# Use lags of blocks that go through DRAM, and the order of token-major products, in a two-layer hybrid trunk

## The chip, the core and the metric

The kernel runs on one core of one Trainium2 chip, in one launch. The metric is the device time in microseconds (us) from the start to the end of the program. TensorE (PE in the profile; its weight loads are PEld) multiplies, VectorE (DVE), ScalarE (ACT) and GpSimd (POOL) do the elementwise work, SyncE (SP) issues most DMAs. Each engine works through its own queue in order.

## What is computed

A trunk of two layers on 256 tokens of width 2048, in fp32. Cut to what matters:

```
h = x
for i in range(2):
    hn = rmsnorm(h, norm[i])
    if i == 0:                       # even layer
        u = hn @ e_w_in              # 2048 x 6144
        ya = head_rmsnorm(hgrn2(q, f, v), a_norm) * silu(za)   # gated linear recurrence, 8 heads
        yb = rg_lru(causal_conv(xb)) * silu(zb)                # 1024 channels
        mix = concat(ya, yb) @ e_w_out                         # 2048 x 2048
    else:                            # odd layer
        u = hn @ o_w_in              # 2048 x 8208
        yc = head_rmsnorm(mlstm(silu(conv(q, k)), v, gates), c_norm)
        mix = (yc * sigmoid(og) * silu(z)) @ o_w_out           # 2048 x 2048
    h = h + mix
    pl = rmsnorm(p[i] @ ple_w[i], ple_norm[i])
    h = h + sigmoid(h @ ple_gate_w[i]) * pl                    # 2048 x 2048
return rmsnorm(h, final_norm)
```

Nearly all the arithmetic is in the products with large weight matrices.

## The kernel before

**Products.** Each fp32 operand is split into two parts of a shorter format (fp32r): `hi` is a cast and `lo` the rest. A product takes three matmuls: hi x hi, hi x lo, lo x hi. The weights are split on the fly. `load_weights` (L119) takes a tile of 128 x 2048, in two halves of 1024 columns: SP loads `raw` (5 buffers), ACT casts it to `whi` (L131), DVE subtracts to get `wlo` (L132). `whi` and `wlo` have 4 buffers each, so two tiles of weights are ready or in work at a time. The split instructions have a raised priority.

There are two layouts. `block` (L154) makes a feature-major result of 128 features x 256 tokens: 32 products per block, one bank of PSUM, the weights stationary. `quarter_tok` (L214) is a quarter of a token-major chunk of 512 features x 256 tokens: the activations are stationary (128 x 128), the weights stream by (512 columns), and there are two accumulators, one for each half of the tokens (`hf`). A quarter `kq` covers four blocks of the contraction (`kk`, 128 rows each), and kk 0, 1 lie in the first half of the weight tile, kk 2, 3 in the second. With 2 token halves, 4 blocks and 3 matmuls that is 24 matmuls of 512 columns per quarter, 96 per chunk. Before the change both halves of a quarter run one after the other: all of hf 0, then all of hf 1. The result of block k and of its activations sits in `act[k // 2]`, an entry for two blocks of the contraction; such entries come from a pool `ap` with 12 buffers, tag `ahl`.

`project_tok` (L190) runs a chunk's four quarters in order. `project_two` (L199) runs the first two chunks of a stage together, in the order (0,0), (0,1), (0,2), (1,0), (1,1), (1,2), (0,3), (1,3) of (chunk, quarter), so that the last quarter of the contraction is needed late. The accumulators of `project_tok` and of the first chunk of `project_two` come from the PSUM pool `pm` (3 banks, tag `mm`); those of the second chunk come from `px` (3 banks, tag `mx`), which small products share. A chunk takes two banks. The token-major stages, in order, with their chunks: ei 2, ez 2 and eo 4 (even layer), g0 4 (its embedding gate), ov 4, oog 4, oz 4, oo 4 (odd layer), g1 3 (its embedding gate, whose last chunk is made otherwise, L1167). That is 31 chunks. g0, ov and g1 begin with `project_two`.

**What reads the accumulators.** ei: ACT L772. ez and oz: ACT L556, then DVE L557. eo and oo: DVE L420. g0: ACT L432. ov: ACT L976. oog: ACT L1096. g1: ACT L1146. The projected embeddings ahead of ei and of oo (`embed`, L317) are evicted by L347 and L349.

**Turning blocks from token-major to feature-major.** A result that becomes the next stage's input must be transposed. `to_features` (L377) and `feature_major` (L515) do this for a chunk of 512 features: DVE transposes 32 x 32 squares (L382, L520), then `across` (L504) writes the tile to DRAM on POOL's queue (L507) and reads it back in four pieces that put the squares in place (L510); after that ACT and DVE scale and split it (L390, L398, L400, L527, L145, L146). `to_features` serves the residual stream: names dfe (after eo, read by g0), dfg (after g0, read by ov and the stages behind it) and dfo (after oo, read by g1). `feature_major` serves the mixer's output: duan (two chunks of the even layer, read by eo) and ducn (three of the odd layer, read by oo; the fourth is transposed by PE).

**The order of work.** Side work is written as generators in named lanes. `pump` (L74) moves each lane one step on, and puts what the step issues behind the latest matmul, cast, subtraction and hop on the queue of each engine (`issue_after`). `quarter_tok` pumps once, in its middle, after 12 matmuls; `block` once, between L161 and L167. `across` ends with `lag` empty steps, so the use of a block stands that many pumps behind its departure. Where a stage must have an entry, `ready` (L406) steps the lane until it is there, and `drain` (L81) runs a lane to its end. Within these bounds a scheduler lays out each queue at build time, by priority and by when it takes operands to be ready.

In the even layer the second `feature_major` (lane fm1) starts ahead of the second gate block pair (`gate_mul`, L849, which evicts through L299 to L305); eo's second quarter reads its entries y[2] and y[3]. In `out_proj` (L413) and `ple_gate` (L425) the last block's entries are read by the quarters (0,3) and (1,3) of the next stage's `project_two`. `ple_gain` (L371, POOL's L374) runs in a lane during eo.

Of the kernel before, what the change touches and what calls it, by code (L numbers as in the profile page):

```python
# [22 lines left out]
KT = D // P  # L23
# [20 lines left out]
def trunk(ctx: ExitStack, tc: tile.TileContext, a, out):  # L44
    nc = tc.nc
    v, s, gp, te, sy = nc.vector, nc.scalar, nc.gpsimd, nc.tensor, nc.sync
# [14 lines left out]
    last = {}  # L61
# [12 lines left out]
    def pump():  # L74
        with ExitStack() as behind:
            for ins in last.values():
                behind.enter_context(tc.issue_after(ins))
            for lane in list(lanes):
                step(lane)
# [31 lines left out]
    def pc(name, i=0, n=None):  # L111
        o, w = PRM[name]
        return prm[:, o + i:o + i + (n or 1)]
# [5 lines left out]
    def load_weights(src, pieces=(1, 1), queues=(sy,)):  # L119
        parts = []  # L120
        for hf in range(2):
            raw = wp.tile([P, 1024], F32, name="raw", tag="raw", bufs=5)
            hi = wp.tile([P, 1024], F32R, name="whi", tag="whi")
            lo = wp.tile([P, 1024], F32R, name="wlo", tag="wlo")
            n = 1024 // pieces[hf]
            for c in range(0, 1024, n):
                r, h, l = (x[:, c:c + n] for x in (raw, hi, lo))
                queues[c // n % len(queues)].dma_start(out=r, in_=src[:, hf * 1024 + c:hf * 1024 + c + n])
                with ExitStack() as order:
                    order.enter_context(tc.high_priority(offset=400))  # L130
                    last["act"] = s.copy(h, r).ins  # L131
                    last["dve"] = v.tensor_tensor(out=l, in0=r, in1=h.bitcast(F32), op=ALU.subtract).ins  # L132
            parts.append((hi, lo))
        return parts

    def act_pair():

        x = ap.tile([P, 1024], F32R, name="ahl", tag="ahl")
        x4 = x.rearrange("p (k i t) -> p k i t", i=2, k=2)
        return x4[:, :, 0], x4[:, :, 1], x  # L140

    def split_act(src, name):
        hi, lo, both = act_pair()
        src = src.rearrange("p (k t) -> p k t", k=2)
        (v.tensor_copy if name == "p0" else s.copy)(hi, src)  # L145
        v.tensor_tensor(out=lo, in0=src, in1=hi.bitcast(F32), op=ALU.subtract)  # L146
        return hi, lo, both
# [39 lines left out]
    def tokens(x, k, hf):  # L187
        return x[:, k, hf * P:(hf + 1) * P]

    def project_tok(w, j, act, before=None):  # L190

        ps = [pm.tile([P, 512], F32, name="mm", tag="mm") for _ in range(2)]
        for kq in range(4):
            if before is not None:
                before(kq)
            quarter_tok(w, j, kq, act, ps)
        return ps
# [16 lines left out]
    def quarter_tok(w, j, kq, act, ps):  # L214

        parts = load_weights(w[4 * j + kq])
        for hf in range(2):
            for kk in range(4):
                k = kq * 4 + kk
                hi, lo = parts[kk // 2]  # L220
                c = (kk % 2) * 512
                ah, al, _ = act[k // 2]
                xh, xl = (tokens(x, k % 2, hf) for x in (ah, al))
                wh, wl = hi[:, c:c + 512], lo[:, c:c + 512]
                te.matmul(ps[hf], xh, wh, start=(k == 0), stop=False)  # L225
                te.matmul(ps[hf], xh, wl, start=False, stop=False)  # L226
                last["pe"] = te.matmul(ps[hf], xl, wh, start=False, stop=(k == KT - 1)).ins  # L227
            if hf == 0:
                pump()

    def newton(y, t, r, yh):
# [145 lines left out]
    def to_features(h, c, act, gain, name, more=None):  # L377

        w = room("w")
        w5 = w.rearrange("p (j c h t) -> p h c j t", j=4, c=4, h=2)  # L380
        for hf in range(2):
            v.transpose(w5[:, hf], h[:, hf].rearrange("p (c j q) -> p c j q", c=4, j=4))  # L382
        r = room("r")
        yield from across(w, r, f"d{name}{c}", 5)
        r5 = r.rearrange("p (i c h t) -> p c h i t", i=4, c=4, h=2)
        for b in range(2):
            if gain:
                x = tp.tile([P, 512], F32, name="xr", tag="hn", bufs=3)
                for k in range(2):
                    s.activation(x[:, k * T:(k + 1) * T].rearrange("p (h i t) -> p h i t", h=2, i=4), r5[:, 2 * b + k],  # L390
                                 AF.Copy, scale=pc(gain, 4 * c + 2 * b + k))
                act[2 * c + b] = split_act(x, "h")
            else:
                hi, lo, both = act_pair()
                for k in range(2):
                    src = r5[:, 2 * b + k]
                    hk, lk = (x[:, k].rearrange("p (h i t) -> p h i t", h=2, i=4) for x in (hi, lo))
                    s.copy(hk, src)  # L398
                    for hf in range(2):
                        v.tensor_tensor(out=lk[:, hf], in0=src[:, hf], in1=hk[:, hf].bitcast(F32), op=ALU.subtract)  # L400
                act[2 * c + b] = (hi, lo, both)
        if more is not None:
            yield
            more(c, r5)
# [8 lines left out]
    def out_proj(hq, w, y, lane):  # L413

        act = {}
        for c in range(4):
            ps = project_tok(w, c, y)
            with tc.high_priority(offset=100):
                for hf in range(2):
                    v.tensor_tensor(out=hq[c][:, hf], in0=ps[hf], in1=hq[c][:, hf], op=ALU.add)  # L420
            start(f"{lane}{c}", to_features(hq[c], c, act, None, lane))
            step(f"{lane}{c}")
        return act
# [80 lines left out]
    def across(w, r, name, lag):  # L504

        d = dr.tile([P, 1024], F32, name=name)
        gp.dma_start(out=d, in_=w)  # L507
        to = r.rearrange("p (i n) -> p i n", i=4)
        for j in range(4):
            last["hop"] = gp.dma_start(out=to[32 * j:32 * j + 32],  # L510
                                       in_=d.rearrange("(i q) (j n) -> j q i n", i=4, j=4)[j]).ins
        for _ in range(lag):
            yield

    def feature_major(u, gain, first, y, room):  # L515

        w = room("w")
        w5 = w.rearrange("p (j c h t) -> p h c j t", j=4, c=4, h=2)
        for hf in range(2):
            v.transpose(w5[:, hf], u[:, hf].rearrange("p (c j q) -> p c j q", c=4, j=4))  # L520
        r = room("r")
        yield from across(w, r, f"du{gain}{first}", 3)
        r5 = r.rearrange("p (i c h t) -> p c h i t", i=4, c=4, h=2)
        for b in range(2):
            x = tp.tile([P, 512], F32, name="xr", tag="hn", bufs=3)
            for k in range(2):
                s.activation(x[:, k * T:(k + 1) * T].rearrange("p (h i t) -> p h i t", h=2, i=4), r5[:, 2 * b + k],  # L527
                             AF.Copy, scale=pc(gain, first + 2 * b + k))
            y[first // 2 + b] = split_act(x, "y")
# [75 lines left out]
    with m0_scope:  # L605
        ew = a["ew"]
        fs, qs, ks = [], [], []
        for g in range(2):
            f = m0.tile([P, 1024], F32, name="f", tag="f")
            k = m0.tile([P, 1024], F32, name="k", tag="k")  # L610
# [271 lines left out]
        def combine():  # L882
            for g in [g for g in held if ("o", g) in res]:
                u = held.pop(g)
                for hf in range(2):
                    v.tensor_tensor(out=u[:, hf], in0=u[:, hf], in1=res["o", g][:, hf], op=ALU.mult)
                start(f"fm{g}", feature_major(u, "an", 4 * g, y, room0))
# [17 lines left out]
    def room(which):  # L905
        return bp.tile([P, 1024], F32, name=which, tag="wt")
# [10 lines left out]
    act = out_proj(hq, a["eo"], y, "fe")  # L917
# [30 lines left out]
    with tc.tile_pool(name="m1", bufs=2) as m1:  # L948
# [143 lines left out]
        for j in range(4):  # L1092
            ps = project_tok(a["oog"], j, acth)
# [10 lines left out]
        for j in range(4):  # L1104
            u = m1.tile([P, 2, 512], F32, name="u", tag="vt", bufs=6)
            gate_tok(a["oz"], j, acth, u)
            for hf in range(2):
                for i in range(2):
                    c = hf * 8 + 2 * j + i
# [28 lines left out]
        act = out_proj(hq, a["oo"], y, "fo")  # L1138
# [54 lines left out]
        for hf, ps in enumerate(quarter(1, [(hf, kq) for hf in range(2) for kq in range(4)])):  # L1193
            pl = pls[3][hf][:, T:2 * T]
            gated(4, ps[hf], hq[3][:, hf, T:2 * T], pl, hf, hf == 0)
            x = hss[:, 4, hf:hf + 1]
            p0 = pre[:, hf:hf + 1]
            y, yh, t, r = (tp.tile([P, 1], F32, name=n, tag=n, bufs=2) for n in ("fy", "fyh", "ft", "fr"))
# [10 lines left out]
            for g, c, n in ((1, 0, 256), (1, 256, 256), (0, 0, 512), (2, 0, 512), (3, 0, 512)):  # L1209
# [13 lines left out]
                x = on.dma_start(out=out[hf * P:(hf + 1) * P, g * 512 + c:g * 512 + c + n], in_=o).ins  # L1223
# [119 lines left out]
```

## Time and profile before

| What | Value |
|---|---|
| median of 3 runs | 1053.65 us (1051.46 to 1054.9) |
| the profiled execution | 1052.88 us |
| its span, first to last instruction | 1051.1 us |
| PE busy, weight loads | 1040.2 us, 876.5 us |
| DVE, ACT, POOL busy | 730.8, 588.6, 140.4 us |
| granted TensorE clock, mean | 0.998 |
| from HBM, to HBM | 209.20 MB, 11.01 MB |

The profile is one execution. A group's row names the line, the engine, the operation, what is written and read, and how many there are; then the busy time, the mean of one in ns, the engine's idle time just before them and what ended it. A row of waits says who waited for whom: total, times, longest. A row of the chain or of a timeline begins with the start and the duration in us; matmuls overlap in the pipeline, so that the step from start to start, not the duration, is PE's pace. A row of windows has the stretch, its length, the busy time of PE, PEld, DVE, ACT and POOL with their instruction counts, then the granted clock, the DMA share and GB/s.

### The profile page before, as it was taken

How to read it: one execution, taken by the hardware profiler on the slowest of the kernel's cores; microseconds unless marked ns; L12 is line 12 of the kernel's file. 1: busy time of each engine (PE TensorE's matmuls, PEld its weight loads, DVE VectorE, ACT ScalarE, POOL GpSimd, SP SyncE). 2: the span in 40 equal slices, each digit the busy share in tenths (PEclk: the TensorE clock that was granted, in tenths of full speed). 3: DMA queues.
4: the chain of work that ended last, by engine and by line, in shares of the span. 5: the costliest groups of instructions: out<-in, count | busy, mean ns of one | idle time of the engine just before them, and what ended most of it. 6: DMA issues, size and time to landing. Idle time of an engine off the chain costs nothing.

```text
span 1051.1 us, 15207 instructions
## 1 busy us (share of the span) xinstructions
PE 1040.2 (99%) x5632; PEld 876.5 (83%) x5632; DVE 730.8 (70%) x1077; ACT 588.6 (56%) x885; POOL 140.4 (13%) x166
## 2 busy tenths in 40 slices
PE   9999999999999999999999999999999999999996
PEld 7888888888888788878888888888888888888886
DVE  7856897997876765767544887764457775665676
ACT  7675545869654444565544656654445565444453
POOL 0001232522204211111000000000001113211021
PEclk9999999999999999999999999999999999999999
DMA  9856454545877777686656444545657785877552
GB/s 357 304 204 200 162 176 146 181 161 182 271 249 257 234 250 230 210 278 219 193 196 200 168 155 159 170 161 193 199 190 223 249 267 183 292 241 245 200 181 81
DMA packets 63242, 221.21 MB, mean 210 GB/s; under 512 B 7744, under 2 KB 9024, under 8 KB 63168
## 3 DMA queue, kind: packets, MB, share of 16 engines
q1 hardware_dynamic: 55440, 196.38, 56.1%
q0 software_dynamic: 7152, 23.07, 7.2%
q8 instruction: 44, 0.72, 0.3%
q10 hardware_dynamic: 576, 0.79, 0.2%
q14 instruction: 30, 0.25, 0.1%
HBM read 209.20 MB, written 11.01 MB: 210 GB/s over the span
## 4 chain that ended last, share of the span: by engine, by line
PE 98%; DVE 1%; DMA 0%; ACT 0%; SPq 0%; issue 0%; ACTq 0%
PE mm L225 19%; PE mm L226 19%; PE mm L227 19%; PE mm L161 17%; PE mm L167 9%; PE mx L225 2%; PE mx L227 2%; PE mx L226 2%; PE mm L338 2%; PE mm L1178 1%; PE mm L1177 1%; PE mm L1176 1%; PE mx L823 1%; PE nu L1059 1%; DVE wlo L132 1%; PE mx L661 0%
## 5 line engine op out<-in xcount | busy, mean ns | idle before, releaser
L132 DVE TENSOR_TENSOR wlo<-raw,whi 128x1024 fp32r<-128x1024 f32 (+1 forms) x364 | 450.4, 1253 | 241.3 <-ACT whi L131 203.5
L131 ACT CAST whi<-raw 128x1024 fp32r<-128x1024 f32 (+1 forms) x364 | 378.0, 1043 | 346.7 <-PE mm L227 232.0
L225 PE MATMUL mm<-whi,ahl 128*128 128x512 f32 x896 | 350.2, 391 | 0.0
L226 PE MATMUL mm<-wlo,ahl 128*128 128x512 f32 x896 | 348.6, 389 | 0.9 <-DVE wlo L132 0.9
L227 PE MATMUL mm<-whi,ahl 128*128 128x512 f32 x896 | 348.5, 389 | 0.0
L225 PEld LDWEIGHTS mm<-whi,ahl 128*128 128x128 f32 x896 | 168.2, 188 | 36.2 <-issue 0.8
L226 PEld LDWEIGHTS mm<-wlo,ahl 128*128 128x128 f32 x896 | 168.2, 188 | 35.8 <-DVE wlo L132 1.3
L227 PEld LDWEIGHTS mm<-whi,ahl 128*128 128x128 f32 x896 | 168.2, 188 | 35.1
L161 PE MATMUL mm<-ahl,whi 128*128 128x512 f32 x768 | 183.1, 390 | 0.0
L161 PEld LDWEIGHTS mm<-ahl,whi 128*128 128x128 f32 x768 | 141.3, 188 | 27.5
L167 PE MATMUL mm<-ahl,wlo 128*128 128x256 f32 x768 | 102.1, 286 | 0.0
L167 PEld LDWEIGHTS mm<-ahl,wlo 128*128 128x128 f32 x768 | 97.2, 191 | 3.6 <-issue 0.4
L507 POOL DMA_DIRECT2D ducn<-w x3 | 1.7, 562 | 329.9 <-DVE w L520 329.9
L225 PE MATMUL mx<-whi,ahl 128*128 128x512 f32 x96 | 37.7, 392 | 0.0
L227 PE MATMUL mx<-whi,ahl 128*128 128x512 f32 x96 | 37.4, 389 | 0.0
L226 PE MATMUL mx<-wlo,ahl 128*128 128x512 f32 x96 | 37.4, 389 | 0.0
L173 ACT COPY sm<-mm 128x256 f32<-128x256 f32 x48 | 17.6, 367 | 31.6 <-PE mm L167 31.6
L961 DVE SCALAR_TENSOR_TENSOR qk<-mg,prm,qk 128x255 f32<-128x255 f32 (+2 forms) x48 | 21.1, 477 | 4.8 <-ACT qk L958 4.5
L225 PEld LDWEIGHTS mx<-whi,ahl 128*128 128x128 f32 x96 | 18.0, 188 | 4.1 <-issue 0.4
L227 PEld LDWEIGHTS mx<-whi,ahl 128*128 128x128 f32 x96 | 18.0, 188 | 3.8
L226 PEld LDWEIGHTS mx<-wlo,ahl 128*128 128x128 f32 x96 | 18.0, 188 | 3.7
L174 DVE TENSOR_TENSOR mg<-mm,sm 128x256 f32<-128x256 f32 x48 | 19.9, 416 | 0.1
(299 smaller groups left out, 886.7 us busy)
## 6 DMA issues: line engine op xcount, KB each, us to landing
raw<-in_ew_dram SPq DMA_DIRECT2D x64, 512.0 KB, 4.3
raw<-in_g_dram SPq DMA_DIRECT2D x56, 512.0 KB, 4.9
raw<-in_eo_dram SPq DMA_DIRECT2D x32, 512.0 KB, 4.9
raw<-in_ov_dram SPq DMA_DIRECT2D x32, 512.0 KB, 4.0
raw<-in_oqk_dram SPq DMA_DIRECT2D x32, 512.0 KB, 4.1
raw<-in_oog_dram SPq DMA_DIRECT2D x32, 512.0 KB, 3.8
raw<-in_oz_dram SPq DMA_DIRECT2D x32, 512.0 KB, 4.4
raw<-in_oo_dram SPq DMA_DIRECT2D x32, 512.0 KB, 4.4
```

The source lines that it names most:

```text
L131: last["act"] = s.copy(h, r).ins
L132: last["dve"] = v.tensor_tensor(out=l, in0=r, in1=h.bitcast(F32), op=ALU.subtract).ins
L161: last["pe"] = te.matmul(ps, parts[k // 8][0][:, c:c + P], act[k // 2][2][:, (k % 2) * 512:(k % 2 + 1) * 512], start=(k == 0), stop=False).ins
L167: last["pe"] = te.matmul(ps[:, T:2 * T], parts[k // 8][1][:, c:c + P], act[k // 2][0][:, k % 2], start=False, stop=(k == KT - 1)).ins
L173: s.copy(small, ps[:, T:2 * T])
L174: v.tensor_tensor(out=dst, in0=ps[:, 0:T], in1=small, op=ALU.add)
L225: te.matmul(ps[hf], xh, wh, start=(k == 0), stop=False)
L226: te.matmul(ps[hf], xh, wl, start=False, stop=False)
L227: last["pe"] = te.matmul(ps[hf], xl, wh, start=False, stop=(k == KT - 1)).ins
L338: last["pe"] = te.matmul(ps[hf], tokens(pact[x], k, hf), (hi, lo)[y][:, k * 512:(k + 1) * 512], start=(n == mine[0]), stop=(n == mine[-1]) ...
L823: te.matmul(ps[:, i * T:(i + 1) * T], bw[:, w, c * P:(c + 1) * P], xc[:, c * T:(c + 1) * T], start=True, stop=True)
L961: v.scalar_tensor_tensor(dst[:, sh:T], pi[:, 0:T - sh], pc("ccw", k * 16 + b), dst[:, sh:T], op0=ALU.mult, op1=ALU.add)
```

## The change

Three edits. In `quarter_tok`, the quarters kq 0, 1 and 2 of each chunk run by block of the contraction: for each kk, first hf 0 and then hf 1. The fourth quarter keeps the old order. The pump stays after 12 matmuls. In `to_features` the lag is 6 instead of 5, in `feature_major` 5 instead of 3.

```diff
     def quarter_tok(w, j, kq, act, ps):
 
         parts = load_weights(w[4 * j + kq])
-        for hf in range(2):
-            for kk in range(4):
-                k = kq * 4 + kk
-                hi, lo = parts[kk // 2]
-                c = (kk % 2) * 512
-                ah, al, _ = act[k // 2]
-                xh, xl = (tokens(x, k % 2, hf) for x in (ah, al))
-                wh, wl = hi[:, c:c + 512], lo[:, c:c + 512]
-                te.matmul(ps[hf], xh, wh, start=(k == 0), stop=False)
-                te.matmul(ps[hf], xh, wl, start=False, stop=False)
-                last["pe"] = te.matmul(ps[hf], xl, wh, start=False, stop=(k == KT - 1)).ins
-            if hf == 0:
+        pairs = [(hf, kk) for hf in range(2) for kk in range(4)]
+        if kq < 3:
+            pairs.sort(key=lambda x: x[1])
+        for n, (hf, kk) in enumerate(pairs):
+            k = kq * 4 + kk
+            hi, lo = parts[kk // 2]
+            c = (kk % 2) * 512
+            ah, al, _ = act[k // 2]
+            xh, xl = (tokens(x, k % 2, hf) for x in (ah, al))
+            wh, wl = hi[:, c:c + 512], lo[:, c:c + 512]
+            te.matmul(ps[hf], xh, wh, start=(k == 0), stop=False)
+            te.matmul(ps[hf], xh, wl, start=False, stop=False)
+            last["pe"] = te.matmul(ps[hf], xl, wh, start=False, stop=(k == KT - 1)).ins
+            if n == 3:
                 pump()
@@ def to_features
-        yield from across(w, r, f"d{name}{c}", 5)
+        yield from across(w, r, f"d{name}{c}", 6)
@@ def feature_major
-        yield from across(w, r, f"du{gain}{first}", 3)
+        yield from across(w, r, f"du{gain}{first}", 5)
```

## The prediction

> **What bounds the kernel now.** First the page: the shares of the engines (section 1), the head of the chain (section 4) and one group (section 5). Then PE's own waits, and windows that end where PE ends.
>
> ```profile
> span 1051.1 us, 15207 instructions
> PE 1040.2 (99%) x5632; PEld 876.5 (83%) x5632; DVE 730.8 (70%) x1077; ACT 588.6 (56%) x885; POOL 140.4 (13%) x166
> PE 98%; DVE 1%; DMA 0%; ACT 0%; SPq 0%; issue 0%; ACTq 0%
> L131 ACT CAST whi<-raw 128x1024 fp32r<-128x1024 f32 (+1 forms) x364 | 378.0, 1043 | 346.7 <-PE mm L227 232.0
> ```
> ```profile
> PE st L95 <- POOL ones L90: 1.1, 1, 1.1
> PE mm L226 <- DVE wlo L132: 0.9, 1, 0.9
> PE mx L338 <- ACT whi L131: 0.3, 1, 0.3
> ```
> ```profile
> 9.00:17.00 8.00, 8.00 (x37) 6.64 (x36) 5.59 (x9) 7.85 (x14) 0.00 (x0) 1.00 1.03 418
> 0.00:1042.50 1042.50, 1040.16 (x5632) 876.45 (x5632) 727.28 (x1066) 585.20 (x879) 140.36 (x166) 1.00 0.64 210
> 1042.50:1051.10 8.60, 0.01 (x1) 0.00 (x0) 3.49 (x12) 3.36 (x6) 0.00 (x0) 0.76 0.66 243
> ```
> TensorE is the bound and nothing else is near it. Its waits sum to 2.3 us; two belong to the start, and the only one inside the kernel is the 0.9 us at L226. The casts on ACT (L131) sat idle 232.0 us until PE gave back a weight buffer: the splitting runs ahead of PE. The tail of 8.6 us holds code that the diff does not touch. A busy PE could still be a slow PE, so I looked at its pace, in the chain and in the timeline of the first 17 us.
>
> ```profile
> 9.12 8.16 PE mm L338 x36
> ...
> 61.27 3.63 PE mm L161 x16
> ```
> ```profile
> 9.87 0.62 PE L338 MATMUL mm<-wlo,ahl 128*128 128x512 f32 x2
> ...
> 12.13 0.62 PE L338 MATMUL mm<-whi,ahl 128*128 128x512 f32 x2
> ```
> The step between 512-column products is 3.63/16 = 0.227 us in a run into one bank, so a quarter (24 products) takes 5.44 us and half of it 2.72. Only stalls can be won: the 0.9 us at L226 and its echo.
>
> **The order of the products.** The count stays 24 per quarter; 31 chunks have 93 reordered quarters. What is added is changes of accumulator: per quarter 8 instead of 2, so 93 x 6 = 558 more. Their price has rows. In the first embedding block (L328 to L330) the pair at 9.87 writes two banks and the pair at 12.13 writes one; both take 0.62. The 36 products of the chain row hold 9 bank changes and average 0.2267 us, no more than the 0.2269 of L161. At the 0.01 us of the print over 9 changes, 558 cost at most 0.6 us or gain as much; I take 0.
>
> **Weight buffers.** Old order: the first half tile (kk 0, 1) comes free after product 18 and the second is needed at product 7. New order: free after 12, needed at 13. Both halves gain 6 x 0.227 = 1.36 us of lead. Lead is worth time only where PE waited, and this is the one wait (chain, groups by line of a window, POOL's and PE's timeline):
>
> ```profile
> 339.87 6.78 DVE wlo L132
> ```
> ```profile
> L132 DVE TENSOR_TENSOR wlo<-raw,whi x4: 1209/1218/6765, 338.5 to 347.7; 128x1024 fp32r<-128x1024 f32 x4
> ```
> ```profile
> 340.49 5.06 POOL L374 TENSOR_TENSOR pl<-pl,row 128x512 f32<-128x512 f32 x4
> ```
> ```profile
> 344.02 0.39 PE L225 MATMUL mm<-whi,ahl 128*128 128x512 f32 x1
> ...
> 345.38 0.39 PE L225 MATMUL mm<-whi,ahl 128*128 128x512 f32 x1
> 346.69 0.50 PE L226 MATMUL mm<-wlo,ahl 128*128 128x512 f32 x1 [0.92 <-DVE wlo L132]
> 347.02 0.39 PE L227 MATMUL mm<-whi,ahl 128*128 128x512 f32 x1
> ```
> One wlo took 6.78 us instead of 1.22, ending 1.1 us after POOL's four L374 (340.49 + 5.06 = 345.55). PE lost 346.69 - 345.38 - 0.227 = 1.08 us, and 0.1 more in the echo (347.02 - 346.69 = 0.33). But the stalled quarter, begun at 344.02, is the **fourth** of eo's second chunk: kq == 3 keeps the old order and needs its second half at product 7. That half's buffer comes free at the end of the second quarter in both orders. So I leave this stall where it is: 0. Bounds: 1.2 us gained if POOL's run shifts off the wlo, 1.36 us (one lead) lost if it shifts the other way.
>
> By the Trainium skill, SBUF — State Buffer, section "SBUF: two separate sides", VectorE and GpSimd take their common port pair as an exclusive lock for a whole instruction. The 6.78 us agree with a lock; were the pair shared by rate, this wlo would end sooner and the sum would be 1.2 us lower.
>
> **PSUM.** Here the change costs. A chunk takes two of three mm banks, so its second accumulator is the bank of the previous chunk's first one, free when that half is evicted. It was first written at product 13, now at product 4: 3 x 0.227 = 0.68 us after the chunk's start instead of 2.72. The evictions (ACT and DVE timelines) and the PE rows they must precede:
>
> ```profile
> 16.95 0.60 ACT L349 COPY pl<-mm 128x512 f32<-128x512 f32 x1
> ...
> 39.31 1.27 ACT L772 ACTIVATE vt<-mm,rcr 128x512 f32<-128x512 f32 x2 [0.54 <-DVE rcr L238]
> ```
> ```profile
> 349.44 0.68 DVE L420 TENSOR_TENSOR hq<-mm,hq 128x512 f32<-128x512 f32 x1
> ```
> ```profile
> 722.07 0.69 ACT L1096 ACTIVATE tho<-mm,rth 128x512 f32<-128x512 f32 x1 [1.73 <-PE mm L227]
> ```
> ```profile
> 17.80 0.39 PE L225 MATMUL mm<-whi,ahl 128*128 128x512 f32 x1
> ...
> 39.56 0.39 PE L225 MATMUL mm<-whi,ahl 128*128 128x512 f32 x1
> ```
> ```profile
> 350.68 0.39 PE L225 MATMUL mm<-whi,ahl 128*128 128x512 f32 x1
> ```
> ```profile
> 724.53 0.39 PE L225 MATMUL mm<-whi,ahl 128*128 128x512 f32 x1
> ```
> - Second chunk of ei: product 4 stood at 39.56. L772 waits for the norm's last step on DVE (rcr) and frees the bank at about 40.00 (its first half, 0.69 us from 39.31). With 0.04 us of hand-over, as at L226 (339.87 + 6.78 = 346.65, then 346.69), the stall is 40.04 - 39.56 = **0.48 us**; bounds 0 and 1.5, the norm coming one cast (1.04 us) sooner or later.
> - First chunk of ei: last copy ends at 17.55, product 4 at 17.80: 0.25 to spare, nothing.
> - Third chunk of eo, the tightest that DVE evicts: 350.12 against 350.68 + 0.68 = 351.36; 1.24 to spare. Third chunk of oog, evicted by ACT: 722.76 against 724.53 + 0.68 = 725.21; 2.45 to spare. 0 for these and the rest between them.
>
> **The lags.** No instruction is added; the uses on ACT and DVE move back one pump for to_features, two for feature_major. The DMAs and their issues on POOL stay at the generator's first step. What goes is ACT's waiting for landings:
>
> ```profile
> ACT xr L390 <- DMA r<-dfg: 3.0, 2, 2.3
> ACT xr L527 <- DMA ru<-duan: 2.5, 1, 2.5
> ACT ahl L398 <- DMA r<-dfe: 1.8, 2, 1.0
> ```
> These 7.3 us lie on an engine that PE did not wait for: 0. Behind the waiting ACT stood the next cast, which has its lead. The later use must still reach PE in time. Tightest of to_features is the last block before ov's (0,3); of feature_major, the even layer's second:
>
> ```profile
> 500.16 1.06 ACT L131 CAST whi<-raw 128x1024 fp32r<-128x1024 f32 x1 [0.30 <-PE mm L227]
> 503.51 1.31 ACT L390 ACTIVATE xr<-r,prm 128x256 f32<-128x256 f32 x3 [2.29 <-DMA r<-dfg]
> ```
> ```profile
> 506.55 0.69 DVE L146 TENSOR_TENSOR ahl<-xr,ahl 128x512 fp32r<-128x512 f32 x1 [0.49 <-ACT ahl L145]
> ```
> ```profile
> 515.49 0.40 PE L225 MATMUL mx<-whi,ahl 128*128 128x512 f32 x1
> ```
> ```profile
> 307.49 0.68 DVE L146 TENSOR_TENSOR ahl<-xr,ahl 128x512 fp32r<-128x512 f32 x1
> ...
> 315.15 0.43 DVE L305 TENSOR_TENSOR ahl<-th,ahl 128x256 fp32r<-128x256 f32 x1 [0.47 <-ACT ahl L304]
> ```
> ```profile
> 311.38 0.39 PE L225 MATMUL mm<-whi,ahl 128*128 128x512 f32 x1
> ```
> ov: the use queues behind a cast, one quarter later: 500.16 + 1.06 + 5.44 = 506.66, plus the 3.73 us from 503.51 to 507.24, is 510.4; (0,3) starts at 515.49. 5 us to spare. Even layer: y[3] was, as I read it, already held to 307.49 for want of an `ahl` slot (12, of which acth fills 8 until the last gate block). Two blocks later y[2] gets there too; both then end about 308.9 (two subtractions of 0.69), and eo's second quarter starts at 311.38: 2.5 us to spare. Cost 0; upper end in the third rival.
>
> **Sum.** 0 + 0 + 0.48 + 0 + 0 = +0.48 us. The profiled execution took 1052.88 us (span 1051.1 plus 1.8 around it), so 1053.4 there. The runs' median is 1053.65, 0.77 above it; on that basis **1054.1 us**.
>
> **Rivals.**
> 1. The stall at L226 vanishes (POOL shifts): -1.2 + 0.48, 1052.9. For: one POOL run on one wlo. Against: both stand behind steps that do not move. Chance 0.10.
> 2. Slower: an eviction on DVE stands behind a wlo that POOL has blocked. It decides once the eviction comes more than 1.24 us late at a chunk's fourth product. The wlo above was 5.56 us late (6.78 - 1.22); at eo's chunk change PE would lose 5.56 - 1.24 = 4.3: 1058.4. For: POOL and L420 both work there, and DVE is 70% busy. Against: it takes a hit on the quarter's very end. Chance 0.08.
> 3. y[2] is put behind the last gate block: 315.15 + 0.43 + 0.69 = 316.27 against 311.38, 4.9 us: 1059.0. Against: its place in the code is before that block's end. Chance 0.05.
> 4. The bank changes cost clock. In the trace the clock stood at 1.00 from 9 to 17 us, across the alternating block. Were it granted at 0.76 (the tail's row, the lowest here) in 93 x 5.44 = 506 us: 506/0.76 - 506 = +160 us, 1214. The Trainium skill, TensorE: Matmul & The Clock Gate, section "A second HAM failure mode: psum-queue depth-cycling", tells of a kernel whose cycling through banks left small gaps that made the clock swing; no row here shows it. Chance 0.01.
> 5. The lags do nothing, because the queues put the uses where they were: the same sum, 1054.1, with ACT's 7.3 us of waits still there. Chance 0.04.
>
> **How the numbers follow.** Forecast 0.70 (rival 5 apart), rivals as above, 0.02 for a gain that I see no source of. 0.3%, about what a measurement of this kernel can tell from no change, is 3.2 us. Forecast, 1 and 5 stay within it (0.84); 2, 3 and 4 are slower (0.14); 0.02 faster. Range: below, rival 1 with 0.6 us for bank changes and the runs' own scatter (1052.9 - 0.6 - 0.7) gives 1051.6; above, the forecast with the ends 1.5 and 1.36 and 0.6 (1053.65 + 3.46) gives 1057.1, short of rivals 2 to 4.
>
> **What would show it.** After: PE still 99%; steps of 0.227 us in quarters that alternate banks (step one); the wait at L226 near 346 (two); a new wait of about 0.5 us at L225 near 39.6, ended by L772 (three); no wait of ACT L390, L527, L398 for landings (four). It is wrong if PE's waits in all grow by several us, or if PE's step or clock changes.

## The result, and the profile after

The changed kernel takes **1055.87 us** (median of 17 runs, 1054.4 to 1060.13); the kernel before, run beside it, takes 1053.08 us (17 runs, 1051.46 to 1057.44). The ratio is 1.0032, with a 95% interval of 1.0024 to 1.0040. So the change costs 2.8 us by the medians and 3.4 us by the ratio. (In the experiments below a ratio can show a gain up to 3 us larger than the medians do: 12 of the 87 executions of the kernel before that ran beside them took more than 1058 us, which moves the ratio and hardly the median.) The time lies inside the range that was given, right at the bound between "within 0.3%" and "slower", and 1.8 us above the forecast of 1054.1.

The profiled execution of the changed kernel took 1055.78 us. The rows below are from its page (sections 1 and 4). From `quarter_tok` on, a line of the kernel before has a number higher by 2 here: L225 to L227 became L227 to L229, L338 became L340, L556 became L558.

```profile
span 1054.0 us, 15212 instructions
PE 1041.1 (99%) x5632; PEld 876.6 (83%) x5632; DVE 731.4 (69%) x1077; ACT 588.1 (56%) x885; POOL 140.2 (13%) x166
PE 96%; ACT 2%; DMA 1%; DVE 1%; issue 0%; POOL 0%; ACTq 0%; POOLq 0%
```

TensorE is still busy 99% of the time. But on the chain that ended last, PE went from 98% to 96%, and ACT and DMA, which had 0%, now have 2% and 1%. A share of 2% is some 20 us of chain, far more than what was lost: the chain only says that PE was no longer alone in setting the end. The next view, PE's waits in the changed kernel, says where.

```profile
PE mm L340 <- ACT pl L351: 1.5, 1, 1.5
PE st L95 <- POOL ones L90: 1.1, 1, 1.1
PE mm L340 <- DVE u L559: 0.6, 1, 0.6
PE mm L228 <- DVE wlo L132: 0.6, 1, 0.6
PE mx L825 <- ACT sq L792: 0.6, 1, 0.6
```

Three of the five are new: two at L340, which is `embed`, and one at L825, small products of the even layer's gates. The wait of 0.5 us at the second chunk of ei isn't there. To turn the waits into a budget, I compared the start of the same product in both traces, at a few landmarks.

| Landmark | before | after | difference | since the landmark above |
|---|---|---|---|---|
| first product of the first quarter | 17.12 | 16.86 | -0.26 | -0.26 |
| L161 after the even layer's gates | 261.41 | 262.05 | +0.64 | **+0.90** |
| the product that waits for wlo near 346 | 346.69 | 347.01 | +0.32 | -0.32 |
| first product of the odd layer's embedding | 855.09 | 855.45 | +0.36 | +0.04 |
| first product of oo | 866.87 | 869.84 | +2.97 | **+2.61** |
| end of the last product | 1042.51 | 1045.47 | +2.95 | -0.02 |

Two places make the loss, and the stall of the weights near 346 got a little shorter. Between the landmarks the traces differ only by small products that changed places with large ones.

**The embedding of the odd layer.** Here are PE's timeline and ACT's timeline of the changed kernel, then ACT's of the kernel before, all around 850 to 860 us.

```profile
857.61 0.50 PE L340 MATMUL mm<-whi,ahl 128*128 128x512 f32 x1 [0.64 <-DVE u L559]
...
860.73 0.50 PE L340 MATMUL mm<-whi,ahl 128*128 128x512 f32 x1 [1.46 <-ACT pl L351]
```
```profile
854.42 1.31 ACT L529 ACTIVATE xr<-r,prm 128x256 f32<-128x256 f32 x3 [3.15 <-DMA r<-ducn]
855.64 0.60 ACT L145 CAST ahl<-xr 128x512 fp32r<-128x512 f32 x1
856.14 0.68 ACT L558 ACTIVATE u<-mm,rth 128x512 f32<-128x512 f32 x1
...
859.53 0.68 ACT L558 ACTIVATE u<-mm,rth 128x512 f32<-128x512 f32 x1
860.11 0.57 ACT L351 COPY pl<-mm 128x512 f32<-128x512 f32 x1
```
```profile
851.30 1.31 ACT L527 ACTIVATE xr<-r,prm 128x256 f32<-128x256 f32 x3 [0.39 <-DMA r<-ducn]
...
853.43 0.67 ACT L556 ACTIVATE u<-mm,rth 128x512 f32<-128x512 f32 x1
```

Read the two ACT timelines against each other. In both, the use of a mixer block (L527, now L529) stands in ACT's queue in front of the eviction of oz's last chunk (L556, now L558), and ACT works its queue in order. Before, the block had landed 0.39 us after ACT came to it. After, ACT stood 3.15 us. The eviction behind it came 2.71 us later (856.14 against 853.43), and DVE's L559, which reads the same bank after it, came later too. The rest of the block's use and two casts then went ahead of the second L558 (859.53) and of L351 (860.11). So PE got its bank late twice: 857.61 is 0.80 us later than the step of 0.227 allows, 860.73 is 1.63 us later, and each has 0.11 us of echo. That makes 2.65 us.

The changed kernel's chain of waits, in a window of this stretch, shows the same from the other side: it runs from PE through ACT into the last piece of that block.

```profile
847.45 6.86 DMA r<-ducn
...
854.42 0.99 ACT xr L529 x3
...
860.73 6.43 PE mm L340 x27
```

Why was the block late? It departed late. DVE's timelines, changed kernel first, show two instructions that changed places.

```profile
837.92 1.22 DVE L132 TENSOR_TENSOR wlo<-raw,whi 128x1024 fp32r<-128x1024 f32 x1
839.06 0.70 DVE L522 STREAM_TRANSPOSE w<-u 128x512 f32<-128x512 f32 x1
```
```profile
837.90 0.71 DVE L520 STREAM_TRANSPOSE w<-u 128x512 f32<-128x512 f32 x1
838.70 1.23 DVE L132 TENSOR_TENSOR wlo<-raw,whi 128x1024 fp32r<-128x1024 f32 x1
```

The new order gives back the first half of a weight tile after product 12 instead of 18. Cast and subtraction have a raised priority, and so the `wlo` now goes ahead of the block's last transpose. In POOL's timeline the departure moved from 838.91 to 840.06. The write then took 5.2 us instead of 4.2 and the last piece read 6.9 instead of 5.9, so that it landed at 854.31 instead of 851.20.

**The gates of the even layer.** The same early cast, another queue. ACT and PE of the changed kernel, then ACT of the kernel before:

```profile
239.86 1.03 ACT L131 CAST whi<-raw 128x1024 fp32r<-128x1024 f32 x1
240.80 0.57 ACT L789 COPY o<-mx 128x512 f32<-128x512 f32 x1
```
```profile
242.47 1.13 PE L825 MATMUL mx<-xc,bw 128*128 128x256 f32 x4 [0.60 <-ACT sq L792]
```
```profile
239.60 0.57 ACT L787 COPY o<-mx 128x512 f32<-128x512 f32 x1
```

The cast at 239.86 stands ahead of the copy that starts to empty an `mx` bank, the copy comes 1.20 us later, and the small products at 242.47 wait 0.60 us for that bank. No experiment moves this cast alone. But in the kernel with the new order alone (below) the cast is ahead of the copy and the wait is there; in the kernels with the lags alone and with the order in two quarters the cast comes at 244.6, behind the copy, and there is no wait.

### The profile page after: what moved, and what is told of

The parts are those of the page before. It is cut to its first block, busy times and chain, and to the rows that moved or that the text cites. A ratio compares the mean times of both kernels' runs of the same rounds, so it can differ in the third digit from the quotient of the medians.

```text
span 1054.0 us, 15212 instructions
## 1 busy us (share of the span) xinstructions
PE 1041.1 (99%) x5632; PEld 876.6 (83%) x5632; DVE 731.4 (69%) x1077; ACT 588.1 (56%) x885; POOL 140.2 (13%) x166
## 4 chain that ended last, share of the span: by engine, by line
PE 96%; ACT 2%; DMA 1%; DVE 1%; issue 0%; POOL 0%; ACTq 0%; POOLq 0%
PE mm L227 19%; PE mm L229 19%; PE mm L228 19%; PE mm L161 17%; PE mm L167 9%; PE mx L229 2%; PE mx L228 2%; PE mx L227 2%; PE mm L340 2%; PE mm L1180 1%; PE mm L1179 1%; PE mm L1178 1%; PE nu L1061 1%; DMA r<-ducn 1%; PE mx L825 1%; DVE wlo L132 1%
## 5 line engine op out<-in xcount | busy, mean ns | idle before, releaser
L227 PE MATMUL mm<-whi,ahl 128*128 128x512 f32 x896 | 350.3, 391 | 0.0
L229 PE MATMUL mm<-whi,ahl 128*128 128x512 f32 x896 | 348.8, 389 | 0.0
L227 PEld LDWEIGHTS mm<-whi,ahl 128*128 128x128 f32 x896 | 168.2, 188 | 36.3 <-issue 1.6
L229 PEld LDWEIGHTS mm<-whi,ahl 128*128 128x128 f32 x896 | 168.2, 188 | 35.1
L161 PE MATMUL mm<-ahl,whi 128*128 128x512 f32 x768 | 183.1, 390 | 0.0
L161 PEld LDWEIGHTS mm<-ahl,whi 128*128 128x128 f32 x768 | 141.3, 188 | 27.5
L227 PE MATMUL mx<-whi,ahl 128*128 128x512 f32 x96 | 37.5, 391 | 0.0
L229 PE MATMUL mx<-whi,ahl 128*128 128x512 f32 x96 | 37.4, 389 | 0.0
L227 PEld LDWEIGHTS mx<-whi,ahl 128*128 128x128 f32 x96 | 18.0, 188 | 3.7
L229 PEld LDWEIGHTS mx<-whi,ahl 128*128 128x128 f32 x96 | 18.0, 188 | 3.7
L340 PE MATMUL mm<-whi,ahl 128*128 128x512 f32 x56 | 18.0, 394 | 2.1 <-ACT pl L351 1.5
```

Source lines behind the costliest of these rows:

```text
L161: last["pe"] = te.matmul(ps, parts[k // 8][0][:, c:c + P], act[k // 2][2][:, (k % 2) * 512:(k % 2 + 1) * 512], start=(k == 0), stop=False).ins
L340: last["pe"] = te.matmul(ps[hf], tokens(pact[x], k, hf), (hi, lo)[y][:, k * 512:(k + 1) * 512], start=(n == mine[0]), stop=(n == mine[-1]) ...
```

## The experiments

The theory that I took into them: the order of the products moves casts and departures; a use that waits for a landing in ACT's queue, in front of an eviction, turns that into PE's time; the longer lags take uses out from in front of evictions, but not the third mixer block's. The rivals: the order itself slows PE (bank changes, or the second bank needed earlier); POOL's blocked subtractions do it; or the lags cost something of their own. "Before" is the kernel before, run beside each experiment on the same chip; its medians there were 1053.02, 1052.87 and 1052.85 us. All intervals are 95%.

### The order alone, and the lags alone

The order alone puts the lags of the changed kernel back:

```diff
-        yield from across(w, r, f"d{name}{c}", 6)
+        yield from across(w, r, f"d{name}{c}", 5)
-        yield from across(w, r, f"du{gain}{first}", 5)
+        yield from across(w, r, f"du{gain}{first}", 3)
```

> The new order of products alone, lags 5 and 3 as before. Theory A (the earlier casts put a wlo ahead of the transposes of oz's third chunk, so its block lands about 3 us later than in the kernel before, while its use stands in ACT's queue at or ahead of the eviction of oz's last chunk, which the next embedding's products need): PE waits 2 to 4 us in the embedding near 857, ratio 1.002 to 1.004. Theory B (the lag of 5 is at fault, since it moves this use out of the last pump and into the drain): no wait there, ratio 0.999 to 1.0005.

Measured: **1062.76 us** (6 runs, 1058.83 to 1065.63), ratio 1.0078, interval 1.0047 to 1.0108. The profiled execution was the fastest one, so the others can have longer waits. PE's longest waits and ACT's waits for mixer blocks in it:

```profile
PE mm L227 <- DVE u L559: 2.2, 2, 1.9
PE mm L340 <- ACT pl L351: 2.0, 1, 2.0
```
```profile
ACT xr L529 <- DMA r<-ducn: 11.0, 3, 4.7
```

The lags alone are the same two lines, 6 and 5, in the kernel before with its old order.

> The lags 6 and 5 alone, old order of products. Theory A: the block leaves and lands as in the kernel before, no wait of PE in the embedding beyond 0.5 us, ratio 0.9995 to 1.001. Theory B: the 2.4 us of PE waits near 857 and 861 are here, ratio 1.002 to 1.004.

Measured: **1051.93 us** (12 runs, 1051.33 to 1053.21), ratio 0.9978, interval 0.9958 to 0.9997. PE has no wait left but those of the start. The third mixer block still stands in front of the eviction in ACT's queue, but there it has all but landed (ACT waits 0.16 us):

```profile
850.08 1.31 ACT L527 ACTIVATE xr<-r,prm 128x256 f32<-128x256 f32 x3 [0.16 <-DMA r<-ducn]
...
852.22 0.67 ACT L556 ACTIVATE u<-mm,rth 128x512 f32<-128x512 f32 x1
```

What follows: the change is two opposed parts. By the ratio and by the medians, the order costs 8 to 10 us by itself, more than twice what I expected. On top of the lags it costs about 4 us by the medians (1055.87 - 1051.93) and between 5 and 6 by the ratios. The lags are what makes the order bearable. In the order alone all three mixer blocks were late in front of evictions. PE's longest wait there, 2.05 us, is in the embedding again; the longest within oz is at 836.89: PE came to a chunk's fourth product, the first one for the second bank, and stood 1.92 us for the eviction (L559). That is the place of my second rival, but what was late in front of the eviction was a landing (834.57), not a subtraction blocked by POOL.

The lags by themselves take off 1.1 us by the medians and 2.3 by the ratio, more than theory A had. The two profiled executions don't show that this comes from uses: PE's products start 0.12 us later than in the kernel before at the first quarter, 0.95 us sooner behind the place near 346, and end 1.01 us sooner. All of the gain is the stall of the weights at that place, which is missing here; the last section says what POOL did then.

### The order in two quarters of each chunk

```diff
-        if kq < 3:
+        if kq in (1, 2):
```

with lags of 5 and 3 as before. The first quarter of a chunk then needs its second bank at product 13 again.

> The new order of products in quarters 1 and 2 of each chunk only, lags 5 and 3 as before: the second accumulator is again first written at product 13. Theory of the early bank (with the order alone, PE waited at the fourth product of a chunk, near 813 and 837, for DVE's eviction): these waits go, the wait for evictions in the embedding stays or shrinks with the departure, ratio 1.001 to 1.004 against 1.0078 for the order in three quarters. Rival (the earlier casts and wlo alone do the harm): waits of 2 us and more stay in oz, ratio 1.005 to 1.008.

Measured: 1057.55 us (12 runs, 1054.77 to 1062.02), ratio 1.0039, interval 1.0024 to 1.0054. The waits at L227 within oz are gone, though ACT still waits for all three mixer blocks (9.7 us in all), so the earlier need of the second bank, which kq 0 alone brings, is what made PE feel the late evictions there. The wait at L825 in the gates is gone too. What stays is the embedding, whose own order did not change, with the longest wait of the study: the last piece of the third block landed at 855.69. PE's timeline and windows around it:

```profile
855.95 0.39 PE L340 MATMUL mm<-whi,ahl 128*128 128x512 f32 x1
859.36 0.62 PE L340 MATMUL mm<-whi,ahl 128*128 128x512 f32 x1 [3.02 <-DVE u L559]
859.79 0.63 PE L340 MATMUL mm<-wlo,ahl 128*128 128x512 f32 x1
```
```profile
856.00:859.30 3.30, 0.34 (x2) 0.00 (x0) 1.37 (x3) 3.30 (x8) 0.00 (x0) 1.00 1.00 410
859.30:862.90 3.60, 3.54 (x8) 2.35 (x9) 3.60 (x6) 3.49 (x5) 0.00 (x0) 0.54 0.15 35
```

Behind this wait the step is 0.43 us instead of 0.227: the granted clock fell to 0.54 in the 3.6 us after it. More on that at the end.

### The third block's use held back

In the changed kernel, the third block's scaling and splitting are put behind the embedding's last copy on ACT; nothing else changes.

```diff
-                            s.copy(pl, ps[hf])
+                            evict["pl"] = s.copy(pl, ps[hf]).ins
...
-        drain("fm0", "fm1", "fm2", "fm3")
+        drain("fm0", "fm1")
+        with tc.issue_after(evict["pl"]):
+            drain("fm2")
+        drain("fm3")
```

> The changed kernel, but the use of the odd layer's third block is queued on ACT behind the embedding's last copy out of PSUM. Both theories: PE's 2.1 us of waits for evictions in the embedding and their echoes go, 2.4 to 2.8 us less than the changed kernel, ratio to the kernel before 0.9995 to 1.001; the block is needed about 10 us later, so no new wait. If the stall has another cause than the queue in front of the evictions, the ratio stays at 1.002 to 1.004.

Measured: **1052.71 us** (12 runs, 1052.02 to 1053.71), ratio 0.9984, interval 0.9965 to 1.0003. The block landed even later than in the changed kernel (855.51), and cost nothing, since its use stood at 866.28 on ACT and the eviction waited for PE alone:

```profile
853.55 0.69 ACT L558 ACTIVATE u<-mm,rth 128x512 f32<-128x512 f32 x1 [1.67 <-PE mm L229]
...
866.28 1.31 ACT L529 ACTIVATE xr<-r,prm 128x256 f32<-128x256 f32 x3
```

Both waits in the odd layer's embedding are gone, and 3.2 us of the medians with them. (The profiled execution was the longest of the twelve; it has a wait of 1.3 us at L340 in the first embedding, near 8 us, which is none of the two.) This is the experiment that carries the study: the same order, the same lags, a later landing, and no loss once nothing stands behind the use that PE needs.

### The transposes ahead of the subtraction

The changed kernel with the `wlo` queued behind the mixer block's transposes on DVE, which undoes the exchange shown above.

```diff
+                    if "w" in gone:
+                        order.enter_context(tc.issue_after(gone["w"]))
...
-            v.transpose(w5[:, hf], u[:, hf].rearrange("p (c j q) -> p c j q", c=4, j=4))
+            gone["w"] = v.transpose(w5[:, hf], u[:, hf].rearrange("p (c j q) -> p c j q", c=4, j=4)).ins
```

> The changed kernel, but the subtractions that make wlo are queued on DVE behind the transposes of feature_major that were issued before them, so the block leaves first. Theory A: the departure is 1 to 1.5 us earlier, the landing too, and PE's waits in the embedding shrink by as much or more: ratio 1.0005 to 1.002. Theory B: the departure does not matter for where the use stands; 1.002 to 1.004.

Measured: 1055.83 us (12 runs, 1054.55 to 1057.67), ratio 1.0020, interval 1.0004 to 1.0036. This was mostly a miss. The block departed 2.0 us sooner (838.02) and landed 2.1 us sooner (852.20), and the two waits in the embedding went from 0.6 and 1.5 us to 0.7 and 0.5 us; but the median did not move, and the ratio fell only within the two intervals. ACT's queue had changed with it:

```profile
852.30 0.91 ACT L531 ACTIVATE xr<-r,prm 128x256 f32<-128x256 f32 x2 [3.94 <-DMA r<-ducn]
853.12 1.03 ACT L131 CAST whi<-raw 128x1024 fp32r<-128x1024 f32 x1
...
856.04 0.68 ACT L560 ACTIVATE u<-mm,rth 128x512 f32<-128x512 f32 x1
```

ACT came to the use one cast sooner, so it waited longer for it (3.94 us against 3.15). Then a weight cast and the whole use stood ahead of the eviction, where in the changed kernel only a part of the use did. The eviction started at 856.04, against 856.14. So the departure is not the whole of it. What counts is everything that stands in front of an eviction in ACT's queue.

### A bank change at every product

The kernel with the third block held, but in quarters 0 to 2 the two token halves take turns product by product: 24 changes of bank per quarter instead of 8, 1488 more in all.

```diff
...
+                for i in range(3):
+                    for o, (x, y) in ((0, other[i]), (1, terms[i])):
+                        last["pe"] = te.matmul(ps[o], x, y, start=(k == 0 and i == 0), stop=False).ins
...
```

> The changed kernel with the held use, and the accumulators changed at every product in quarters 0 to 2: 24 changes of bank per quarter instead of 8, 1488 more. If a change of bank costs nothing: PE's step stays 0.227 us, ratio 0.998 to 1.002 (the second bank is needed 0.45 us earlier, which may cost up to 1 us). If it costs 0.01 us: 15 us more, ratio 1.012 to 1.016. If the clock swings from it: the granted clock under 0.98 and 50 us or more.

Measured: 1053.13 us (12 runs, 1052.68 to 1055.01), ratio 0.9993, interval 0.9979 to 1.0008; clock 0.997. Its chain of waits in oog has three whole quarters in one piece, each product in another bank than the one before:

```profile
702.86 16.32 PE mm L234 x72
719.18 5.44 PE mm L237 x24
```

16.32/72 = 0.2267 us, and 5.44/24 = 0.2267 us in the fourth quarter, which changes banks once. So changing the bank cost nothing here, and the clock stayed at 0.997. The rival with slower products is out.

### The lag of to_features alone

```diff
-        yield from across(w, r, f"d{name}{c}", 5)
+        yield from across(w, r, f"d{name}{c}", 6)
```

in the kernel before.

> The kernel before with the lag of to_features at 6 alone. Theory of the race (the 1.1 us at L226 near 346 hangs on whether a wlo starts just ahead of POOL's run of four or inside it, and the lag only shifts the two by chance): the wait may be there or not; ratio 0.998 to 1.0005 either way. Theory that this lag removes the wait: it is gone, ratio 0.9975 to 0.9992.

Measured: 1052.26 us (12 runs, 1051.4 to 1054.99), ratio 0.9976, interval 0.9955 to 0.9998. The stall near 346 stands (1.1 us of wait at L226, before 0.9), so the lag does not remove it. The ratio is that of both lags together, and the median is 0.3 us above theirs: these runs can't tell what the lag of `feature_major` adds in the old order.

### POOL's products in one run, with either lag of to_features

The first of these two was meant for the stall near 346: without POOL's four products near 340 it should go. In the kernel before, `ple_gain` gives way once per two of its products, so that here POOL runs eight of them in one go (15.95 us) ahead of the first dfe block, which then leaves at 338.10 instead of 332.27.

```diff
-                yield
+            yield
```

> The kernel before with POOL's eight gain products in one run ahead of the first block's reads, instead of four before and four behind them. Theory (one wlo that starts just before such a run is blocked for all of it): no POOL product near 340, so the wait of 0.9 us at L226 near 346 goes, and no other comes if no wlo starts just before the run: ratio 0.9980 to 0.9995. If a wlo is caught ahead of the eight, PE waits 3 to 6 us near 330 instead: 1.002 to 1.005.

Measured: 1054.39 us (12 runs, 1053.05 to 1057.99), ratio 1.0012, interval 0.9998 to 1.0026. The stall near 346 is gone, as expected, but the time is a miss: PE waits at 353.79 instead, by 1.6 us. ACT's and DVE's timelines show the same pattern as in the embedding: a use waits for a landing, and DVE's part of it stands in front of L420, an eviction.

```profile
352.01 1.32 ACT L398 CAST ahl<-r 128x256 fp32r<-128x256 f32 x4 [6.90 <-DMA r<-dfe]
```
```profile
352.44 0.69 DVE L400 TENSOR_TENSOR ahl<-r,ahl 128x128 fp32r<-128x128 f32 x3 [6.08 <-ACT ahl L398]
353.06 0.68 DVE L420 TENSOR_TENSOR hq<-mm,hq 128x512 f32<-128x512 f32 x1
```

So the late departure made the same loss in another stage. If it does so only through what its use stands in front of, a longer lag must remove it. The same kernel with the lag of `to_features` at 6:

> The kernel before with POOL's eight products in two runs of eight ahead of the first residual block (as in the run before) and the lag of to_features at 6. With lag 5 the first dfe block left at 338.1 us, its use stood in ACT ahead of DVE's L420, and PE waited 1.6 us at 353.79. Theory A (a wait of PE appears when a use reaches its queue before its block has landed, and the lag buys one pump, half a quarter or more): the departure stays at 338, the use moves back by at least 2.7 us, and the wait near 353.8 shrinks below 0.4 us or vanishes; 1052 to 1053 us, 1.5 us or more under the same kernel with lag 5. Rival (POOL's blocked subtraction makes the wait, the landing is by the way): the wait stays above 1 us and the time at 1054.

Measured: 1052.04 us (12 runs, 1051.31 to 1065.14), ratio 1.0003, interval 0.9968 to 1.0039. The wait at 353.79 is gone from the profile, and the median fell by 2.4 us; the two intervals overlap, so it is the trace that shows it. The departure stayed (338.17). DVE's timeline shows both evictions of the chunk ahead of the use:

```profile
346.94 0.69 DVE L420 TENSOR_TENSOR hq<-mm,hq 128x512 f32<-128x512 f32 x1 [0.41 <-PE mm L227]
...
350.52 0.68 DVE L420 TENSOR_TENSOR hq<-mm,hq 128x512 f32<-128x512 f32 x1
...
352.88 1.66 DVE L400 TENSOR_TENSOR ahl<-r,ahl 128x128 fp32r<-128x128 f32 x8
```

The block also landed 1.6 us sooner here (350.23 against 351.83), by chance as far as I can tell; but the first L420 had run at 346.94 and the second at 350.52, and neither would have cared. The move of the use itself was smaller than expected: two casts went ahead of it on ACT, and it began 1.4 us earlier than the one with lag 5 that had stood waiting.

### Both lags and the hold, in the old order

The best of the parts: the old order, lags 6 and 5, third block held.

> The old order of products, both lags (6 and 5), and the use of the third mixer block held behind the embedding's last copy on ACT. Theory A (the lags gain by taking uses out from in front of evictions, and the third block is the one that they leave there): in the old order the third block departs earlier (838.2 against 840.1 in the changed kernel) and lands at about 850, before its place in ACT's queue, so nothing is left to hold: the same time as the lags alone, 1051.9 us, ratio 0.997 to 0.999, and no PE wait at L340 in the embedding of the odd layer. Rival (the hold itself costs, since the block's split then stands late before oo): 0.5 us or more above the lags alone, 1052.5 or later, with a PE wait at the start of oo.

Measured: **1052.15 us** (12 runs, 1051.27 to 1053.12), ratio 0.9969, interval 0.9945 to 0.9992. PE's only wait is the 1.1 us of the very start. The hold costs nothing and gains nothing there, as the theory had it. This kernel and the lags alone are both a little shorter than the kernel before (0.7 and 1.1 us by the medians) and than the changed one. Against the same kernel in the new order (1052.71) it is 0.56 us shorter; by the budget above the new order is worth +0.90 - 0.32 = +0.58 us outside the embedding. The intervals of the two ratios overlap, and the stall near 346 is in that kernel's profile and not in this one's, so the agreement shows little.

## Why the prediction held in its range and failed in its sum

The sum was +0.48 us; the profiles show +2.95 us of PE. That the time fell into the range is luck: the upper end was made of bounds on the bank of ei, the stall near 346 and the bank changes, none of which was needed, and the loss came from steps that had been put at 0. Step by step:

- **Order of the products, price of a bank change: right.** I took 0 within 0.6 us, and the kernel with 1488 more changes shows 0.2267 us per product in both kinds of quarter.
- **Weight buffers: right in place, half seen.** The stall stayed in the fourth quarter, at 0.60 us of wait instead of 0.92, within the bounds of 1.2 us gained and 1.36 us lost. But I counted 1.36 us of lead per half tile as "worth time only where PE waited" and stopped there. The lead also lets casts and subtractions with a raised priority run earlier, in front of other work. That cost 0.90 us around the gates (L825), and it put the third block's departure behind a `wlo`. I worked out what the products need and not what the released buffers trigger.
- **PSUM: the 0.48 us did not come, its place was another.** The norm came about 0.9 us sooner (L774 starts at 38.42, where L772 stood at 39.31), the bank was free before the fourth product, and the lower bound of 0 held. Why the norm came sooner is open. I had looked only from chunk to chunk; the changeover that lost time is from oz to the embedding, whose own order is unchanged.
- **The lags: the 0 that failed.** The step put ACT's waits for landings at 0, because they "lie on an engine that PE did not wait for", took the departures as fixed, and named the even layer's second block as the tightest of `feature_major`. The tight one was the odd layer's third, whose 0.39 us of wait at 851.30 the step left out. The prediction asked if the later use reaches PE in time, and never if the block has landed when ACT comes to the use, and what stands behind it. With the order's earlier `wlo` the block departed later, the 0.39 us became 3.15, and PE lost 2.61 us. Of the four signs that were to show the forecast, two came (the step of 0.227, the wait near 346), the wait near 39.6 did not, and the fourth failed here: ACT waits for a landing at L529, formerly L527. As the price of the lags alone, 0 is not refuted: they lose nothing, and the 1.0 us that they gain between the profiles lies at the stall near 346.
- **The rivals.** The first did not come in the changed kernel; it came with the lags alone, where POOL's four products and the `wlo` took turns. The second came nearest. Its place, a chunk's fourth product with a late eviction, is where the order alone lost 2.08 us; its cause, a subtraction blocked by POOL, was not what the trace showed. Of the third there is no sign: PE has no wait near 311. The fourth (the clock) is out by the kernel with the most bank changes. The fifth is wrong: the waits of ACT for dfe, dfg and duan went with the lags, as forecast.

What of this is shown: that the two waits in the embedding come from the third block's use in front of L558 (the hold removes both, 3.2 us), that the lags take off most of what the order costs (5 to 7 us), that bank changes cost nothing. Shown by the traces, with times that only agree: that the lag of `to_features` removes the wait at 353.79. Only argued: that the cast at 239.86 makes the 0.90 us at the gates; what the lags gain in the old order; and that the departure was late because of the exchanged `wlo`, in this size. Undoing the exchange brought the departure back, but the same transfer also took 1 us longer in each direction in the changed kernel, and why it did is open.

## What to carry to other kernels

On an engine that works in order, an instruction that can wait for a DMA is a price on everything queued behind it: look for evictions behind uses, however idle the engine is on average, and either hold the use until after the eviction or give the transfer more time. Buffers that come free earlier are not only slack; work with a raised priority will take the time, and pushes back whatever shared its queue. A tuned order and its lags are one thing: here one part cost 8 to 10 us alone, the other gained 1 to 2 alone, and both together cost 3.

## What was new about the hardware

**Behind a wait of 3 us the clock was granted at half.** In the kernel with the order in two quarters PE waited 3.02 us, and the eight products behind that wait took 3.71 us from 859.36 to 863.07 instead of 8 x 0.227 = 1.82, at a granted clock of 0.54 in the window shown above; then the clock was 1.00 again. (About 0.2 us of the difference is a second wait, for L351.) It is one wait in one execution. The order alone had waits of 1.92 and 2.05 us and the changed kernel one of 1.46, and the clock stayed at 1.00 behind all three. The Trainium skill, TensorE: Matmul & The Clock Gate, section "Why this matters for your kernels", advises "No PE-idle gaps >~3µs between matmul bursts" and says that one idle window brings the clock back to half; these traces agree on both sides of that figure.

**POOL against DVE.** A run of four products on POOL (L374 in the kernel before) near 340 us took one of two forms. In the kernel before and in eight others it ran through in 5.05 or 5.06 us, and one `wlo` on DVE was held until about 1 us after its end, for up to 6.9 us. In the kernel with the lags alone the same four were stretched, with DVE's `wlo` at 2.10 us in between, and PE did not wait:

```profile
339.77 7.08 POOL L374 TENSOR_TENSOR pl<-pl,row 128x512 f32<-128x512 f32 x4
```

The four products near 321 us were stretched to 6.9 us or more in all ten of these kernels. Three kernels in which the `wlo` near 340 started after POOL's run were held just the same, so who starts first does not decide it; what does stays open. The prediction read the 6.78 us of its `wlo` as agreeing with a lock for a whole instruction. One L374 takes 1.3 us, so that explains 1.3 of the 5.56 us at most: what the traces show is a hold over a run of four.
